# Rotary embedding on one core: both products of a chunk in one VectorE operation, and four units stored in two transfers of 64 partitions

## Chip, cores and metric

One core of a Trainium2 chip. The metric is device time in microseconds (us); lower is better. A run's time is some 2 us longer than the span that its profile shows (85.87 against 83.8 in the profiled run of before).

## The reference

```python
batch, n_heads, seq, head_dim = (8, 8, 1024, 64)        # fp32
x_first, x_second = x[..., :32], x[..., 32:]
out_first  = x_first * cos_cached - x_second * sin_cached
out_second = x_first * sin_cached + x_second * cos_cached
```

The input is 16.8 MB and the output another 16.8 MB. Every element is read once, takes part in two products and one sum, and is written once.

## The kernel before

The data is cut into eight units of 2 MB, each 128 partitions by 64 rows of 64 values (16 KB per partition). All eight loads go out at the start, on SyncE's queue, and the stores follow on the same queue in the order 0, 1, 3, 2, 4, 5, 6, 7. ScalarE copies a chunk of 24 or 16 rows into PSUM (`st`). VectorE multiplies the copy by the sines into `s` and by the cosines into `x`. The sums are shared out: TensorE (accumulating in PSUM, copied back by ScalarE), GpSimd, or VectorE itself in the chunks called `alone`. GpSimd does unit 2 alone.

```python
xt = [xp.tile([P, F], fp32, name=f"x{u}") for u in range(n_u)]
# ... cut: unit 0 is loaded in two halves of its columns
for u in range(1, n_u):
    nc.sync.dma_start(out=xt[u], in_=xf[u])
# ... cut
def products(pt, u, n0, n1, alone=False):
    xr, sr, pr = rows(xt[u], n0, n1), rows(s_of(u), n0, n1), rows(pt, 0, n1 - n0)
    mul(nc.vector, sr, pr, tab(sn, n0, n1))
    mul(nc.vector, pr if alone else xr, pr, tab(cs, n0, n1))
    if alone:
        sums(nc.vector, xr, pr, sr)

def store(u, n0=0, n1=R):
    nc.sync.dma_start(out=of[u][:, n0 * hd:n1 * hd], in_=xt[u][:, n0 * hd:n1 * hd])
# ... cut
for c, (u, n0, n1) in enumerate(chunks):
    products(st[c], u, n0, n1, (u, n0) in alone)
    put(c + 2)                       # ScalarE stages the chunk after next
    if c in back:
        pe_back(*back[c])            # sums of TensorE back into x
    if c in on_pe:
        pe_sums(*on_pe[c])
    for f, *args in behind.get(c, ()):
        f(*args)                     # GpSimd's sums, and the stores
```

Of the kernel before, what the change touches and what calls it, by code (L numbers as in the profile page):

```python
# [8 lines left out]
def kernel(  # L9
# [7 lines left out]
    nc = tc.nc  # L17
    fp32 = mybir.dt.float32
    TT = mybir.AluOpType
    P = nc.NUM_PARTITIONS  # L20

    b, h, seq, hd = x.shape
    half = hd // 2
    R = 64
    F = R * hd
    T = R * half
    n_u = (b * h * seq) // (R * P)
    BK = 512
    G = BK // half
    Q = 32  # L30
    H = R // 2
    C = H * half
# [4 lines left out]
    of = out.rearrange("b h s d -> (b h s d)").rearrange(  # L37
        "(u p m) -> u p m", p=P, m=F)

    ctx.enter_context(tc.manual_schedule())  # L40
    const = ctx.enter_context(tc.tile_pool(name="const", bufs=1))
    xp = ctx.enter_context(tc.tile_pool(name="xp", bufs=1))
    tv = ctx.enter_context(tc.tile_pool(name="tv", bufs=3))
    tg = ctx.enter_context(tc.tile_pool(name="tg", bufs=1))

    cs = const.tile([P, T], fp32, name="cs")
    sn = const.tile([P, T], fp32, name="sn")
    ones = const.tile([P, 2 * P], fp32, name="ones")
    sel, plus = ones[0:Q, :P], ones[:, P:]
    minus = const.tile([P, P], fp32, name="minus")  # L50


    raw = tv.tile([P, F], fp32, name="raw", tag="s")
    rs, rc = raw[0:Q, 0:C], raw[0:Q, C:2 * C]
    nc.sync.dma_start(out=rs, in_=sin_cached.rearrange("(q n) j -> q (n j)", q=Q))
    nc.scalar.dma_start(out=rc, in_=cos_cached.rearrange("(q n) j -> q (n j)", q=Q))


    xt = [xp.tile([P, F], fp32, name=f"x{u}") for u in range(n_u)]
    for m0, m1 in ((0, F // 2), (F // 2, F)):  # L60
        nc.sync.dma_start(out=xt[0][:, m0:m1], in_=xf[0][:, m0:m1])
    for u in range(1, n_u):
# [7 lines left out]
                            channel_multiplier=1)  # L70
    nc.gpsimd.affine_select(out=plus, in_=plus, compare_op=TT.not_equal, fill=1.0,
                            base=0, pattern=[[-1, P]], channel_multiplier=1)
    nc.vector.tensor_scalar_mul(out=minus, in0=plus, scalar1=-1.0)

    def rows(t, n0, n1):
        return t[:, n0 * hd:n1 * hd].rearrange("p (n k j) -> p n k j", k=2, j=half)

    def tab(t, n0, n1):
        v = t[:, n0 * half:n1 * half].rearrange("p (n o j) -> p n o j", o=1, j=half)
        return v.to_broadcast([P, n1 - n0, 2, half])  # L80

    def mul(eng, o, a, t):
        eng.tensor_tensor(out=o, in0=a, in1=t, op=TT.mult)  # L83

    def sums(eng, o, c, s):
        eng.tensor_tensor(out=o[:, :, 0], in0=c[:, :, 0], in1=s[:, :, 1], op=TT.subtract)  # L86
        eng.tensor_tensor(out=o[:, :, 1], in0=c[:, :, 1], in1=s[:, :, 0], op=TT.add)  # L87

    sv = {}

    def s_of(u):
        if u not in sv:
            sv[u] = tv.tile([P, F], fp32, name="s", tag="s")
        return sv[u]

    def stage(pt, u, n0, n1):
        nc.scalar.copy(out=pt[:, :(n1 - n0) * hd], in_=xt[u][:, n0 * hd:n1 * hd])  # L97

    def products(pt, u, n0, n1, alone=False):

        xr, sr, pr = rows(xt[u], n0, n1), rows(s_of(u), n0, n1), rows(pt, 0, n1 - n0)
        mul(nc.vector, sr, pr, tab(sn, n0, n1))
        mul(nc.vector, pr if alone else xr, pr, tab(cs, n0, n1))
        if alone:
            sums(nc.vector, xr, pr, sr)

    def on_pool(u, n0, n1):
        g = tg.tile([P, F // 2], fp32, name="g")
        xr, gr = rows(xt[u], n0, n1), rows(g, 0, n1 - n0)
        mul(nc.gpsimd, gr, xr, tab(sn, n0, n1))  # L110
        mul(nc.gpsimd, xr, xr, tab(cs, n0, n1))
        sums(nc.gpsimd, xr, xr, gr)

    def pool_sums(u, n0, n1):
        xr = rows(xt[u], n0, n1)
        sums(nc.gpsimd, xr, xr, rows(s_of(u), n0, n1))

    def store(u, n0=0, n1=R):
        nc.sync.dma_start(out=of[u][:, n0 * hd:n1 * hd], in_=xt[u][:, n0 * hd:n1 * hd])



# [2 lines left out]
    with ExitStack() as first:  # L125
        p0, p1 = [first.enter_context(tc.tile_pool(name=n, bufs=1, space=PS))
                  for n in ("p0", "p1")]
        en = p0.tile([P, C], fp32, name="en")
        ec = [p0.tile([P, BK], fp32, name=f"ec{i}") for i in range(2)]
        pre = p1.tile([P, 4 * BK], fp32, name="pre")  # L130
        for part, r in ((en[:, :BK], rs[:, :BK]), (en[:, BK:], rs[:, BK:]),
                        (ec[0], rc[:, :BK]), (ec[1], rc[:, BK:])):
            nc.tensor.matmul(part, sel, r, start=True, stop=True)  # L133
        odd = [2 * (i % (Q // 2)) + 1 for i in range(Q)]
        for t, r in ((sn, rs), (cs, rc)):
            nc.vector.stream_shuffle(t[0:Q, C:], r, odd)  # L136
        for t in (sn, cs):
            for k in range(1, P // Q):
                nc.gpsimd.tensor_copy(out=t[k * Q:(k + 1) * Q, C:], in_=t[0:Q, C:])  # L139
        mul(nc.vector, rows(s_of(0), 0, H), rows(xt[0], 0, H), tab(en, 0, H))  # L140
        for i in range(2):
            xr = rows(xt[0], i * G, (i + 1) * G)
            mul(nc.vector, xr, xr, tab(ec[i], 0, G))
        pool_sums(0, 0, H)
        stage(pre, 0, H, R)
        nc.scalar.copy(out=sn[:, :C], in_=en)
        for i in range(2):
            nc.scalar.copy(out=cs[:, i * BK:(i + 1) * BK], in_=ec[i])
        products(pre, 0, H, R)
        pool_sums(0, H, R)  # L150

# [2 lines left out]
    st, acc = {}, {}  # L154

    def pe_sums(u, n0):
        acc[u, n0] = q2.tile([P, 2 * BK], fp32, name="acc")
        a = acc[u, n0].rearrange("p (k n j) -> p k n j", k=2, j=half)
        xr, sr = rows(xt[u], n0, n0 + G), rows(s_of(u), n0, n0 + G)
        for k in range(2):  # L160
            nc.tensor.matmul(a[:, k], plus, xr[:, :, k], start=True, stop=False)  # L161
            nc.tensor.matmul(a[:, k], plus if k else minus, sr[:, :, 1 - k],  # L162
                             start=False, stop=True)

    def pe_back(u, n0):
        a = acc[u, n0].rearrange("p (k n j) -> p n k j", k=2, j=half)
        nc.scalar.copy(out=rows(xt[u], n0, n0 + G), in_=a)  # L167

    on_pool(2, 0, 32)


    cuts = ((0, 24), (24, 48), (48, 64))
    chunks = [(u, n0, n1) for u in (1, 3, 4, 5, 6, 7) for n0, n1 in cuts]
    alone = {(1, 48), (3, 48), (6, 48), (7, 24), (7, 48)}
    on_pe = {0: (1, 0), 1: (1, 16), 3: (3, 0), 4: (3, 16), 6: (3, 32), 8: (4, 0),
             9: (5, 0), 11: (5, 16), 12: (6, 0)}
    back = {1: (1, 0), 3: (1, 16), 4: (3, 0), 6: (3, 16), 8: (3, 32), 9: (4, 0),
            11: (5, 0), 12: (5, 16), 14: (6, 0)}
    behind = {
        1: [(pool_sums, 1, 32, 48), (on_pool, 2, 32, 64)],  # L180
        3: [(store, 1)],
        8: [(store, 3), (store, 2), (pool_sums, 4, 16, 64)],
        9: [(store, 4)],
        11: [(pool_sums, 5, 32, 64)],
        12: [(store, 5)],
        13: [(pool_sums, 6, 16, 48)],
        14: [(store, 6)],
        15: [(pool_sums, 7, 0, 24)],
        16: [(store, 7, 0, 48)],
        17: [(store, 7, 48, 64)],  # L190
    }

    def put(c):
        if c < len(chunks):
            u, n0, n1 = chunks[c]
            st[c] = (q1 if c % 2 else q0).tile([P, 3 * BK], fp32, name="st")
            stage(st[c], u, n0, n1)
# [2 lines left out]
    put(1)  # L200
    store(0)
    for c, (u, n0, n1) in enumerate(chunks):
        products(st[c], u, n0, n1, (u, n0) in alone)
        put(c + 2)
        if c in back:
            pe_back(*back[c])
# [3 lines that stand above are left out]
            f(*args)  # L210
# [29 lines left out]
```

## Time and profile before

| | before |
|---|---|
| time, median of 6 runs | 85.78 us (85.73 to 85.88) |
| span of the profiled run | 83.8 us |
| busy: VectorE, GpSimd, ScalarE | 72.3, 65.9, 37.2 us |
| DMA, share of 16 engines, main queue | 95.7% |
| last VectorE operation ends, last store lands | 77.3, 82.7 us |

Two rows disagree on what the bound is: VectorE is busy 86% of the span and the page's chain of work ends on it, while the DMA engines are busy longer and to the end. In a table of stretches, the last two columns are the mean busy share of the 16 DMA engines and the GB/s they moved. A packet is what the profile records as one piece of a DMA engine's work: of the 2640 in the main queue before, 1792 are the 16 KB that a unit has on one partition.

### The profile page before, as it was taken

The numbers are of one execution on the slowest core, as the hardware profiler recorded it, in microseconds if no ns is written. First come the engines' busy times: TensorE is split into PE (matmuls) and PEld (weight loads), VectorE is DVE, ScalarE is ACT, GpSimd is POOL, SyncE is SP. The second block draws the span as 40 slices with busy tenths as digits, with TensorE's granted clock in tenths as the row PEclk, the third lists the DMA queues.
The fourth block names the chain that finished last, engine by engine and source line by source line (L and its number), as shares of the span: only waits on it lengthen the run. The fifth ranks groups of instructions, "written<-read, shape, count | busy, mean of one in ns | idle before, by whom it ended". The sixth has DMA issues, their size and how long they took to land. (4 is left out here: it accounts for less than half of the span.)

```text
span 83.8 us, 409 instructions
## 1 busy us (share of the span) xinstructions
PE 42.4 (51%) x80; PEld 16.2 (19%) x80; DVE 72.3 (86%) x56; ACT 37.2 (44%) x32; POOL 65.9 (79%) x35
## 2 busy tenths in 40 slices
PE   0299910003994965949469089594959800000000
PEld 0234100002341403314033042231404200000000
DVE  1284999999999999999999999999999999998000
ACT  4100694464066553674636951976346852000000
POOL 5059959999999999999999999999999959400000
PEclk9999999999999999999999999999999999655555
DMA  2999999999999999999999999999999999999990
GB/s 59 309 411 450 415 461 391 461 415 454 415 415 454 399 469 399 446 422 415 352 415 446 415 446 407 462 415 446 422 422 454 399 450 407 462 415 434 417 385 23
DMA packets 2689, 33.83 MB, mean 404 GB/s; under 512 B 320, under 2 KB 320, under 8 KB 512
## 3 DMA queue, kind: packets, MB, share of 16 engines
q1 hardware_dynamic: 2640, 33.69, 95.7%
q10 hardware_dynamic: 48, 0.13, 0.4%
q14 instruction: 1, 0.01, 0.0%
HBM read 17.04 MB, written 16.78 MB: 404 GB/s over the span
## 5 line engine op out<-in xcount | busy, mean ns | idle before, releaser
L97 ACT COPY st<-x 128x1536 f32<-128x1536 f32 (+1 forms) x18 | 23.4, 1302 | 18.2 <-DVE x L83 10.2
L161 PE MATMUL acc<-x,ones 128*128 128x512 f32 x36 | 20.4, 650 | 20.6 <-ACT x L167 11.3
L83 DVE TENSOR_TENSOR s<-st,sn 128x1536 f32<-128x1536 f32 (+1 forms) x18 | 28.2, 1568 | 0.0
L83 DVE TENSOR_TENSOR x<-st,cs 128x1536 f32<-128x1536 f32 (+1 forms) x13 | 21.6, 1663 | 0.0
L86 POOL TENSOR_TENSOR x<-x,s 128x1024 f32<-128x1024 f32 (+3 forms) x7 | 15.8, 2262 | 1.9 <-ACT x L167 0.9
L87 POOL TENSOR_TENSOR x<-x,s 128x1024 f32<-128x1024 f32 (+3 forms) x7 | 15.8, 2258 | 0.0
L161 PEld LDWEIGHTS acc<-x,ones 128*128 128x128 f32 x36 | 6.6, 204 | 33.6 <-ACT x L167 17.9
L167 ACT COPY x<-acc 128x1024 f32<-128x1024 f32 x9 | 9.1, 1010 | 6.5 <-PE acc L162 6.5
L162 PE MATMUL acc<-s,minus 128*128 128x512 f32 x18 | 10.1, 644 | 0.0
L83 POOL TENSOR_TENSOR x<-x,cs 128x2048 f32<-128x2048 f32 x2 | 9.1, 4540 | 0.2
L162 PE MATMUL acc<-s,ones 128*128 128x512 f32 x18 | 9.2, 592 | 0.0
L83 POOL TENSOR_TENSOR g<-x,sn 128x2048 f32<-128x2048 f32 x2 | 9.1, 4532 | 0.0
L83 DVE TENSOR_TENSOR st<-st,cs 128x1024 f32<-128x1024 f32 (+1 forms) x5 | 6.6, 1328 | 0.0
L139 POOL COPY sn<-sn 32x1024 f32<-32x1024 f32 x3 | 3.1, 1032 | 3.4 <-DVE sn L136 3.3
L133 PE MATMUL en<-raw,ones 32*128 32x512 f32 x4 | 3.7, 1089 | 3.7 <-DMA raw<-in_sin_cached_dram 3.7
L86 POOL TENSOR_TENSOR x<-x,g 128x1024 f32<-128x1024 f32 x2 | 4.7, 2350 | 0.2
L97 ACT COPY pre<-x 128x2048 f32<-128x2048 f32 x1 | 1.9, 1870 | 6.6 <-DMA x<-in_x_dram 6.6
L87 POOL TENSOR_TENSOR x<-x,g 128x1024 f32<-128x1024 f32 x2 | 4.7, 2358 | 0.0
L162 PEld LDWEIGHTS acc<-s,minus 128*128 128x128 f32 x18 | 3.7, 206 | 4.9 <-issue 4.9
L162 PEld LDWEIGHTS acc<-s,ones 128*128 128x128 f32 x18 | 3.4, 190 | 4.3 <-issue 4.3
L86 DVE TENSOR_TENSOR x<-st,s 128x512 f32<-128x512 f32 (+1 forms) x5 | 3.7, 745 | 0.2
L87 DVE TENSOR_TENSOR x<-st,s 128x512 f32<-128x512 f32 (+1 forms) x5 | 3.7, 733 | 0.0
(23 smaller groups left out, 25.9 us busy)
## 6 DMA issues: line engine op xcount, KB each, us to landing
x<-in_x_dram SPq DMA_DIRECT2D x7, 2048.0 KB, 24.8
out_dram<-x SPq DMA_DIRECT2D x7, 2048.0 KB, 10.1
x<-in_x_dram SPq DMA_DIRECT2D x2, 1024.0 KB, 6.4
out_dram<-x SPq DMA_DIRECT2D x1, 1536.0 KB, 7.7
out_dram<-x SPq DMA_DIRECT2D x1, 512.0 KB, 5.4
raw<-in_cos_cached_dram ACTq DMA_DIRECT2D x1, 128.0 KB, 3.2
raw<-in_sin_cached_dram SPq DMA_DIRECT2D x1, 128.0 KB, 2.8
```

The source lines that it names most:

```text
L83: eng.tensor_tensor(out=o, in0=a, in1=t, op=TT.mult)
L86: eng.tensor_tensor(out=o[:, :, 0], in0=c[:, :, 0], in1=s[:, :, 1], op=TT.subtract)
L87: eng.tensor_tensor(out=o[:, :, 1], in0=c[:, :, 1], in1=s[:, :, 0], op=TT.add)
L97: nc.scalar.copy(out=pt[:, :(n1 - n0) * hd], in_=xt[u][:, n0 * hd:n1 * hd])
L133: nc.tensor.matmul(part, sel, r, start=True, stop=True)
L139: nc.gpsimd.tensor_copy(out=t[k * Q:(k + 1) * Q, C:], in_=t[0:Q, C:])
L161: nc.tensor.matmul(a[:, k], plus, xr[:, :, k], start=True, stop=False)
L162: nc.tensor.matmul(a[:, k], plus if k else minus, sr[:, :, 1 - k], start=False, stop=True)
L167: nc.scalar.copy(out=rows(xt[u], n0, n0 + G), in_=a)
```

## The change

The intent is to take VectorE's fixed cost per instruction (some 65 ns by the starts in the trace of before: 1.67 us apart at 1536 elements, 1.13 at 1024) once per chunk in place of twice. To let one operation write both products, `x` and `s` of a unit become neighbours in one wide tile, cosine and sine tables are interleaved row by row, and pairs of units share a product buffer. Work is rebalanced: unit 2 goes partly to VectorE, and two of the five `alone` chunks give their sums away. Separately, the first four stores are cut in two. The core of the diff:

```diff
+    for i, (u0, u1) in enumerate(((3, 6), (0, 4), (1, 5))):
+        w = xp.tile([P, 3 * F], fp32, name=f"w{i}")
+        xt[u0], xt[u1] = w[:, :F], w[:, 2 * F:]
+        sv[u0] = sv[u1] = w[:, F:2 * F]
+        px[u0], px[u1] = both(w[:, :2 * F]), both(w[:, F:])[:, :, ::-1]
 ... cut: units 7 and 2, tables, order of the work
-        mul(nc.vector, sr, pr, tab(sn, n0, n1))
-        mul(nc.vector, pr if alone else xr, pr, tab(cs, n0, n1))
+        mul(nc.vector, px[u][:, n0:n1].rearrange("p n t (k j) -> p n t k j", k=2),
+            xr.to_broadcast([P, n, 2, hd]).rearrange("p n t (k j) -> p n t k j", k=2), tr)
 ... cut
-        nc.sync.dma_start(out=of[u][:, n0 * hd:n1 * hd], in_=xt[u][:, n0 * hd:n1 * hd])
+        step = P // 2 if u < 4 else P
+        for p in range(0, P, step):
+            nc.sync.dma_start(out=of[u][p:p + step, n0 * hd:n1 * hd],
+                              in_=xt[u][p:p + step, n0 * hd:n1 * hd])
```

More of the change, by code (lines that the diff above doesn't have):

```diff
@@ L42 @@
     xp = ctx.enter_context(tc.tile_pool(name="xp", bufs=1))
-    tv = ctx.enter_context(tc.tile_pool(name="tv", bufs=3))
-    tg = ctx.enter_context(tc.tile_pool(name="tg", bufs=1))
-    cs = const.tile([P, T], fp32, name="cs")
-    sn = const.tile([P, T], fp32, name="sn")
+    tb = const.tile([P, 2 * T], fp32, name="tb")
+    tb4 = tb.rearrange("p (n t j) -> p n t j", t=2, j=half)
     ones = const.tile([P, 2 * P], fp32, name="ones")
@@ L50, with both @@
     minus = const.tile([P, P], fp32, name="minus")
-    raw = tv.tile([P, F], fp32, name="raw", tag="s")
-    rs, rc = raw[0:Q, 0:C], raw[0:Q, C:2 * C]
+    xt, sv, px = {}, {}, {}
+    def both(t):
+        return t.rearrange("p (w n f) -> p n w f", w=2, f=hd)
+    for i, (u0, u1) in enumerate(((3, 6), (0, 4), (1, 5))):
[3 more added lines that the diff above has]
+        px[u0], px[u1] = both(w[:, :2 * F]), both(w[:, F:])[:, :, ::-1]
+    K = 40
+    w = xp.tile([P, K * hd + F], fp32, name="w3")
+    gt, xt[7] = w[:, :K * hd], w[:, K * hd:]
+    sv[7], px[7] = gt, both(w[:, :2 * K * hd])[:, :, ::-1]
+    xt[2], sv[2] = xp.tile([P, F], fp32, name="x2"), sv[3]
+    rs, rc = sv[3][0:Q, 0:C], sv[3][0:Q, C:2 * C]
     nc.sync.dma_start(out=rs, in_=sin_cached.rearrange("(q n) j -> q (n j)", q=Q))
     nc.scalar.dma_start(out=rc, in_=cos_cached.rearrange("(q n) j -> q (n j)", q=Q))
-    xt = [xp.tile([P, F], fp32, name=f"x{u}") for u in range(n_u)]
     for m0, m1 in ((0, F // 2), (F // 2, F)):
@@ L72 @@
                             base=0, pattern=[[-1, P]], channel_multiplier=1)
-    nc.vector.tensor_scalar_mul(out=minus, in0=plus, scalar1=-1.0)
+    nc.scalar.mul(out=minus, in_=plus, mul=-1.0)
+    cs, sn = tb4[:, :, 0], tb4[:, :, 1]
     def rows(t, n0, n1):
@@ L78, in tab, with flat @@
     def tab(t, n0, n1):
-        v = t[:, n0 * half:n1 * half].rearrange("p (n o j) -> p n o j", o=1, j=half)
-        return v.to_broadcast([P, n1 - n0, 2, half])
+        return t[:, n0:n1].unsqueeze(2).to_broadcast([P, n1 - n0, 2, half])
+    def flat(t):
+        return t.rearrange("p (n j) -> p n j", j=half)
     def mul(eng, o, a, t):
@@ L87, in sums, with products, alone @@
         eng.tensor_tensor(out=o[:, :, 1], in0=c[:, :, 1], in1=s[:, :, 0], op=TT.add)
-    sv = {}
-    def s_of(u):
-        if u not in sv:
-            sv[u] = tv.tile([P, F], fp32, name="s", tag="s")
-        return sv[u]
     def stage(pt, u, n0, n1):
         nc.scalar.copy(out=pt[:, :(n1 - n0) * hd], in_=xt[u][:, n0 * hd:n1 * hd])
-    def products(pt, u, n0, n1, alone=False):
-        xr, sr, pr = rows(xt[u], n0, n1), rows(s_of(u), n0, n1), rows(pt, 0, n1 - n0)
+    def products(pt, u, n0, n1):
+        n = n1 - n0
+        if u not in px:
+            for o, t in ((sv[u], sn), (xt[u], cs)):
+                mul(nc.vector, rows(o, n0, n1), rows(pt, 0, n), tab(t, n0, n1))
+            return
+        xr = pt[:, :n * hd].rearrange("p (n o f) -> p n o f", o=1, f=hd)
+        tr = tb4[:, n0:n1].unsqueeze(3).to_broadcast([P, n, 2, 2, half])
+        mul(nc.vector, px[u][:, n0:n1].rearrange("p n t (k j) -> p n t k j", k=2),
+            xr.to_broadcast([P, n, 2, hd]).rearrange("p n t (k j) -> p n t k j", k=2), tr)
+    def alone(pt, u, n0, n1):
+        s = sv[4] if u == 7 else sv[u]
+        xr, sr, pr = rows(xt[u], n0, n1), rows(s, n0, n1), rows(pt, 0, n1 - n0)
         mul(nc.vector, sr, pr, tab(sn, n0, n1))
-        mul(nc.vector, pr if alone else xr, pr, tab(cs, n0, n1))
-        if alone:
-            sums(nc.vector, xr, pr, sr)
+        mul(nc.vector, pr, pr, tab(cs, n0, n1))
+        sums(nc.vector, xr, pr, sr)
     def on_pool(u, n0, n1):
-        g = tg.tile([P, F // 2], fp32, name="g")
-        xr, gr = rows(xt[u], n0, n1), rows(g, 0, n1 - n0)
+        xr, gr = rows(xt[u], n0, n1), rows(gt, n0, n1)
         mul(nc.gpsimd, gr, xr, tab(sn, n0, n1))
@@ L115, in pool_sums @@
         xr = rows(xt[u], n0, n1)
-        sums(nc.gpsimd, xr, xr, rows(s_of(u), n0, n1))
+        sums(nc.gpsimd, xr, xr, rows(sv[u], n0, n1))
     def store(u, n0=0, n1=R):
-        nc.sync.dma_start(out=of[u][:, n0 * hd:n1 * hd], in_=xt[u][:, n0 * hd:n1 * hd])
+        step = P // 2 if u < 4 else P
+        for p in range(0, P, step):
+            nc.sync.dma_start(out=of[u][p:p + step, n0 * hd:n1 * hd],
+                              in_=xt[u][p:p + step, n0 * hd:n1 * hd])
     PS = bass.MemoryType.PSUM
@@ L135 @@
         for t, r in ((sn, rs), (cs, rc)):
-            nc.vector.stream_shuffle(t[0:Q, C:], r, odd)
-        for t in (sn, cs):
-            for k in range(1, P // Q):
-                nc.gpsimd.tensor_copy(out=t[k * Q:(k + 1) * Q, C:], in_=t[0:Q, C:])
-        mul(nc.vector, rows(s_of(0), 0, H), rows(xt[0], 0, H), tab(en, 0, H))
+            nc.vector.stream_shuffle(t[0:Q, H:], flat(r), odd)
+        for k in range(1, P // Q):
+            nc.gpsimd.tensor_copy(out=tb4[k * Q:(k + 1) * Q, H:], in_=tb4[0:Q, H:])
+        mul(nc.vector, rows(sv[0], 0, H), rows(xt[0], 0, H), tab(flat(en), 0, H))
         for i in range(2):
             xr = rows(xt[0], i * G, (i + 1) * G)
-            mul(nc.vector, xr, xr, tab(ec[i], 0, G))
+            mul(nc.vector, xr, xr, tab(flat(ec[i]), 0, G))
         pool_sums(0, 0, H)
         stage(pre, 0, H, R)
-        nc.scalar.copy(out=sn[:, :C], in_=en)
+        nc.scalar.copy(out=sn[:, :H], in_=flat(en))
         for i in range(2):
-            nc.scalar.copy(out=cs[:, i * BK:(i + 1) * BK], in_=ec[i])
+            nc.scalar.copy(out=cs[:, i * G:(i + 1) * G], in_=flat(ec[i]))
         products(pre, 0, H, R)
@@ L158, in pe_sums @@
         a = acc[u, n0].rearrange("p (k n j) -> p k n j", k=2, j=half)
-        xr, sr = rows(xt[u], n0, n0 + G), rows(s_of(u), n0, n0 + G)
+        xr, sr = rows(xt[u], n0, n0 + G), rows(sv[u], n0, n0 + G)
         for k in range(2):
@@ L167, in pe_back @@
         nc.scalar.copy(out=rows(xt[u], n0, n0 + G), in_=a)
-    on_pool(2, 0, 32)
+    on_pool(2, 0, K // 2)
     cuts = ((0, 24), (24, 48), (48, 64))
     chunks = [(u, n0, n1) for u in (1, 3, 4, 5, 6, 7) for n0, n1 in cuts]
-    alone = {(1, 48), (3, 48), (6, 48), (7, 24), (7, 48)}
-    on_pe = {0: (1, 0), 1: (1, 16), 3: (3, 0), 4: (3, 16), 6: (3, 32), 8: (4, 0),
-             9: (5, 0), 11: (5, 16), 12: (6, 0)}
-    back = {1: (1, 0), 3: (1, 16), 4: (3, 0), 6: (3, 16), 8: (3, 32), 9: (4, 0),
-            11: (5, 0), 12: (5, 16), 14: (6, 0)}
-    behind = {
-        1: [(pool_sums, 1, 32, 48), (on_pool, 2, 32, 64)],
-        3: [(store, 1)],
-        8: [(store, 3), (store, 2), (pool_sums, 4, 16, 64)],
-        9: [(store, 4)],
-        11: [(pool_sums, 5, 32, 64)],
-        12: [(store, 5)],
-        13: [(pool_sums, 6, 16, 48)],
-        14: [(store, 6)],
-        15: [(pool_sums, 7, 0, 24)],
-        16: [(store, 7, 0, 48)],
-        17: [(store, 7, 48, 64)],
+    chunks.insert(9, (2, K, R))
+    whole = {(6, 48), (7, 24), (7, 48)}
+    on_pe = {0: (1, 0), 3: (3, 0), 4: (3, 16), 6: (4, 0), 7: (4, 16), 10: (5, 0),
+             11: (5, 16), 13: (6, 0)}
+    back = {2: (1, 0), 4: (3, 0), 6: (3, 16), 8: (4, 0), 9: (4, 16), 11: (5, 0),
+            13: (5, 16), 15: (6, 0)}
+    behind = {
+        2: [(pool_sums, 1, 16, 64), (store, 1)],
+        5: [(pool_sums, 3, 32, 64), (on_pool, 2, K // 2, K)],
+        6: [(store, 3)],
+        9: [(pool_sums, 2, K, 64), (store, 2), (pool_sums, 4, 32, 64), (store, 4)],
+        12: [(pool_sums, 5, 32, 64)],
+        13: [(store, 5)],
+        14: [(pool_sums, 6, 16, 48)],
+        15: [(store, 6)],
+        16: [(pool_sums, 7, 0, 24)],
+        17: [(store, 7, 0, 48)],
+        18: [(store, 7, 48, 64)],
     }
@@ L202 @@
     for c, (u, n0, n1) in enumerate(chunks):
-        products(st[c], u, n0, n1, (u, n0) in alone)
+        (alone if (u, n0) in whole else products)(st[c], u, n0, n1)
         put(c + 2)
```

## The prediction

A is the rival in which the stores in halves run at half the rate; its "up to 105" is 85.8 + 19.6, and its "95 to 102" stands as the author's guess.

> **What bounds the kernel now.** I read the page's chain of work that ended last first, because it names a culprit, and then tried to refute it.
>
> ```profile
> DVE 38%; issue 2%; DVEq 1%
> DVE s L83 17%; DVE x L83 13%; DVE st L83 5%; DVE x L86 2%; DVE x L87 2%; DVEq L235 1%
> ```
>
> The chain ends on VectorE and never mentions a transfer. Taken at its word, each microsecond saved on VectorE would be a microsecond of the kernel. But the chain only reaches back to 42 us and covers 41% of the span, and VectorE's last operation ends at 77.3 us while the span is 83.8. So I looked at what the transfers do, in the slices and in the queue part of the page.
>
> ```profile
> DVE  1284999999999999999999999999999999998000
> DMA  2999999999999999999999999999999999999990
> GB/s 59 309 411 450 415 461 391 461 415 454 415 415 454 399 469 399 446 422 415 352 415 446 415 446 407 462 415 446 422 422 454 399 450 407 462 415 434 417 385 23
> q1 hardware_dynamic: 2640, 33.69, 95.7%
> HBM read 17.04 MB, written 16.78 MB: 404 GB/s over the span
> ```
>
> Both rows are full, but only the DMA row is full until the end. All loads and all stores are in one queue (q1), which holds 95.7% of the time of 16 engines. The table of stretches gives the rate:
>
> ```profile
> 2.50:37.00 34.50, 20.17 (x32) 7.59 (x32) 31.84 (x25) 15.96 (x14) 30.69 (x16) 1.00 1.02 427
> 37.00:44.00 7.00, 5.16 (x12) 2.18 (x13) 7.00 (x6) 3.59 (x5) 6.92 (x3) 1.00 0.99 396
> 44.00:81.00 37.00, 17.04 (x38) 6.44 (x36) 33.21 (x26) 16.32 (x14) 27.19 (x11) 0.88 1.00 428
> ```
>
> The last two columns are the DMA share and GB/s: 427 while loading, 428 while storing, share 1.0 in both. Last, does the queue ever wait for a store? The time line of SyncE and the waits of the stores, one at a time, give issue and time to landing. The first store is issued at 21.58 us and lands 27.0 us later, because the loads queue ahead of it (the last load, issued at 6.5, lands after 37.1, at 43.6). The last one:
>
> ```profile
> 77.34 0.33 SPq L119 DMA_DIRECT2D out_dram<-x  x1
> DMA to landing us min/median/max: 5.4/5.4/5.4
> ```
>
> Issue plus landing for all nine: unit 0 at 21.6 lands 48.6; 1 at 37.9 lands 53.4; 3 at 48.5 lands 58.2; 2 at 51.7 lands 63.1; 4 at 58.5 lands 68.0; 5 at 63.1 lands 73.0; 6 at 67.8 lands 77.9; 7a at 73.8 lands 81.5; 7b at 77.3 lands 82.7. Whole units land 4.8 to 5.0 us apart (2.10 MB at 428 GB/s is 4.90), and every store is issued 4 us or more before the one ahead of it has landed (the least: 73.8 against 77.9). The queue never runs dry. **The bound is the transfers' rate**, and VectorE is second with about 3 us of slack: 4 us less roughly 1 us from issue to the first byte (the first load is issued at 1.2; traffic is seen from about 2).
>
> [...]starts lie 1.67 us apart at 1536 elements and 1.13 at 1024, so 1.04 to 1.05 ns per element and some 65 ns fixed. [...]each 2 MB transfer spans 128 partitions, and the two 32-partition loads are 128 KB, too small to show a rate.
>
> **The change part by part.**
> VectorE: 15 chunks and the second half of unit 0 become one operation of double length in place of two, 16 x 65 ns = -1.0 us. Two "alone" chunks lose their two sums, 0.69 and 0.68 us with the gap around 1.3: -2.7. One chunk of unit 2 (24 rows) comes over from GpSimd as two operations of 1.67: +3.3. Sum -0.4: the last operation would end near 76.9 instead of 77.3. The negated identity moves to ScalarE: 0.23 us at 1.7 us, where VectorE waited anyway: 0.
> GpSimd: unit 2 costs 4.53 + 4.54 + 2.35 + 2.36 = 13.8 us per 32 rows; 40 rows instead of 64 save 10.3. Its sums grow from 216 to 288 rows, at 2 x 2.34 us per 32 rows: +10.5. Sum about 0. TensorE loses one group of nine and ScalarE one copy out of PSUM (1.0), for one staging copy (1.44): 0.
> Store times by the new order: unit 3 near 42 (behind sums of GpSimd), 2 near 54, 4 near 58.5, 5 near 63, 6 near 68, 7a near 73.2, 7b near 77. Only unit 2 moves back, by 2 us, and it is not wanted before unit 3 has landed, at 58. So the queue still never runs dry, and all of the VectorE part is **worth 0 on the path**.
> Transfers: same bytes. Units 0, 1, 2, 3 take eight transfers in place of four; the four further issues, 0.33 us each on SyncE, lie far ahead of need. So 8.4 MB, or 4 x 4.9 = 19.6 us of the path, run in a new form, and its rate is the one term that can move the time much. If each engine still moves 16 KB rows at its own pace, the term is 0. What could be won is the weak stretch from loads to stores: 37 to 44 us at 396 GB/s instead of 427, 7 x 31/427 = 0.5 us. Half of that, -0.3, is my guess, as someone who split only the first four stores was probably looking there.
> Sum: 85.84 + 0 + 0 - 0.3 = 85.5.
>
> **The rivals.**
> A, [...]19.6 us become up to 39, and since queue time is path time, the kernel would take up to 105 us; [...]less, 95 to 102. Against it: [...]the restriction to four units looks like a choice made after trying. I give it about 1 in 5.
> B, VectorE was the bound after all, as the chain has it. Then the time falls by its 0.4 us: 85.4. Hardly to be told apart from my number; a landing well after issue speaks against it.
> C, a new wait. One fused operation writes two tiles, and units now share product buffers: the chunk of unit 2 (VectorE ready near 42.6) needs the sums of unit 3 done by GpSimd (near 41.7), less than 1 us of margin; if ordering is kept by whole buffers, other chunks might wait too. Waits below 3 us in total vanish in the slack; 5 us would give 88. About 1 in 12. A slower rate of the fused operation, whose output jumps between two regions, would act alike: 10% on 16 operations of 3.2 us is 5 us.
> D, the transition and the end both get tighter: 0.5 us from above, and 0.8 at most from engines that finish unevenly (81 to 82.7 us runs at a falling rate). That gives 84.5. Below 84.1, which 2% takes, there is nothing left to win, as the bytes alone at 428 GB/s take 78.7 us, and the start and the end of the program are unchanged.
>
> **Range and chances.** Between D and a small C lie 84.5 and 87; A lies far outside, and I leave it there. Faster by over 2%: 0.05, as D falls short of it. Slower by over 2%: 0.22, almost all A and some C. Within 2%: 0.73. Predicted 85.5, range 84.4 to 87.2.
>
> **What would show it.** Right: VectorE's last operation near 77, last store's issue near 77, landing near 82.5, DMA share 1.0 and over 420 GB/s in 44 to 64 us, a fused operation of 3072 elements near 3.27 us from start to start. A: in the stretch where units 0 to 3 leave, share near 1.0 at 220 to 300 GB/s, units landing 7 to 10 us apart, GpSimd and VectorE unchanged. C: gaps on VectorE named after GpSimd or TensorE and, only then, DMA slices below 9. The prediction is wrong if the time leaves 2%, and its reasoning is wrong if VectorE ends much earlier and the time follows it.

## The result, and the profile after

The changed kernel takes 99.44 us (median of 6 runs, 97.35 to 101.03) against 85.78: ratio 1.142, 95% interval 1.133 to 1.151. A ratio here is the mean time of one kernel's fast runs over that of the other's fast runs of the same rounds, so not quite the ratio of the medians. The time scatters by 4%, where before it scattered by 0.2%. Runs more than 1.5% above the fastest are labelled slow: four of the six here. The fast ones are 97.35 and 98.64 us; the second is the profiled one (span 96.2).

The prediction's main number was wrong. Its rival A had foreseen 95 to 102 us, at a chance of 1 in 5.

VectorE, transfers and rate in 40 slices, from the page of after (a slice is 2.4 us, 2.1 before):

```profile
DVE  0367999999999999999999999999999910000000
DMA  2999999999999999999979989999999999998410
GB/s 37 381 409 480 436 429 422 422 402 415 429 422 436 436 436 436 436 402 375 252 232 211 347 259 279 354 375 395 286 293 354 415 429 429 412 431 366 208 77 12
```

The DMA row stays full, but the rate falls to between 211 and 395 GB/s from the twentieth slice to the thirtieth (46 to 72 us). That is where units 0 to 3 leave. Then it recovers, and at the very end it fades over four slices where before it stopped in one. The table of stretches of after, columns as in the prediction's:

```profile
2.50:37.00 34.50, 19.12 (x27) 7.17 (x28) 31.56 (x15) 16.64 (x15) 29.81 (x13) 0.97 1.02 427
44.00:60.00 16.00, 11.91 (x26) 4.31 (x24) 16.00 (x7) 10.31 (x10) 15.84 (x9) 1.00 1.01 275
84.00:96.20 12.20, 0.00 (x0) 0.00 (x0) 0.00 (x0) 0.00 (x0) 0.00 (x0) 0.50 0.53 224
```

Loading runs at the old 427 GB/s. From 44 to 60 us the share is 1.01 at 275 GB/s: the engines always have a packet in hand, and the packets are slow. The records of single 16 KB packets say so directly: 0.61 us nearly everywhere before (some thirty of 1792 took up to 1.08 us, most of them at the turn from loads to stores), and a mixture of 0.61, 1.2 and up to 1.5 us here, with four up to 2.7.

From the time line of VectorE and the waits of SyncE, after and then before:

```profile
76.61 0.68 DVE L108 TENSOR_TENSOR w<-st,w 128x512 f32<-128x512 f32 x1
SPq L263 <- DMA out_dram<-w: 17.5, 5, 4.8
```
```profile
SPq L235 <- DMA out_dram<-x: 5.0, 2, 3.8
```

VectorE ends at 77.3 us as before, and the last store is issued at 77.3 as before. It then takes 18.1 us to land instead of 5.4, and SyncE waits 17.5 us for transfers at the end. The end of the computation did not move; the queue behind it did. Whole units, which had landed every 4.9 us, are complete at 50.2, 58.8, 65.8 and 76.0 us (units 0, 1, 3, 2), and from there every 4.8 us again.

Of the 12.4 us of longer span, part is an uneven finish of the engines: in the last 12.2 us they idle 0.47 x 12.2 = 5.7 us on the mean, where the last 7.8 us before had 0.28 x 7.8 = 2.2. That is 3.5 us; the other 8.9 are slower packets.

### The profile page after: what moved, and what is told of

Read it like the earlier page. It is cut to its first block, busy times and chain, and to the rows that moved or that the text cites. A ratio compares the mean times of both kernels' runs of the same rounds, so it can differ in the third digit from the quotient of the medians.

```text
span 96.2 us, 376 instructions
## 1 busy us (share of the span) xinstructions
PE 40.6 (42%) x72; PEld 15.4 (16%) x72; DVE 71.7 (75%) x37; ACT 37.8 (39%) x33; POOL 65.9 (68%) x36
## 5 line engine op out<-in xcount | busy, mean ns | idle before, releaser
L104 DVE TENSOR_TENSOR w<-st,tb 128x3072 f32<-128x3072 f32 (+3 forms) x19 | 50.6, 2727 | 0.0
L111 ACT COPY st<-w 128x1536 f32<-128x1536 f32 (+1 forms) x18 | 23.4, 1302 | 20.6 <-DVE w L104 14.9
L188 PE MATMUL acc<-w,ones 128*128 128x512 f32 x32 | 19.4, 693 | 19.5 <-ACT w L194 10.4
L107 POOL TENSOR_TENSOR w<-w 128x1024 f32<-128x1024 f32 (+2 forms) x8 | 19.3, 2418 | 0.4 <-POOL tb L166 0.4
L108 POOL TENSOR_TENSOR w<-w 128x1024 f32<-128x1024 f32 (+2 forms) x8 | 19.4, 2420 | 0.0
L188 PEld LDWEIGHTS acc<-w,ones 128*128 128x128 f32 x32 | 6.2, 215 | 31.7 <-ACT w L194 16.2
L189 PE MATMUL acc<-w,minus 128*128 128x512 f32 x16 | 10.0, 709 | 0.0
L194 ACT COPY w<-acc 128x1024 f32<-128x1024 f32 x8 | 8.1, 1009 | 3.5 <-PE acc L189 3.4
L189 PE MATMUL acc<-w,ones 128*128 128x512 f32 x16 | 8.2, 592 | 0.0
L104 POOL TENSOR_TENSOR x<-x,tb 128x1280 f32<-128x1280 f32 x2 | 5.8, 2898 | 0.2
L104 POOL TENSOR_TENSOR w<-x,tb 128x1280 f32<-128x1280 f32 x2 | 5.9, 2947 | 0.0
L107 POOL TENSOR_TENSOR x<-x,w 128x640 f32<-128x640 f32 (+1 forms) x3 | 4.9, 1636 | 0.2
L108 POOL TENSOR_TENSOR x<-x,w 128x640 f32<-128x640 f32 (+1 forms) x3 | 4.9, 1636 | 0.0
L189 PEld LDWEIGHTS acc<-w,ones 128*128 128x128 f32 x16 | 3.1, 193 | 4.2 <-issue 4.2
## 6 DMA issues: line engine op xcount, KB each, us to landing
out_dram<-w SPq DMA_DIRECT2D x1, 512.0 KB, 18.1
```

The lines of the kernel that those rows point to most:

```text
L104: eng.tensor_tensor(out=o, in0=a, in1=t, op=TT.mult)
L107: eng.tensor_tensor(out=o[:, :, 0], in0=c[:, :, 0], in1=s[:, :, 1], op=TT.subtract)
L108: eng.tensor_tensor(out=o[:, :, 1], in0=c[:, :, 1], in1=s[:, :, 0], op=TT.add)
L111: nc.scalar.copy(out=pt[:, :(n1 - n0) * hd], in_=xt[u][:, n0 * hd:n1 * hd])
L188: nc.tensor.matmul(a[:, k], plus, xr[:, :, k], start=True, stop=False)
L189: nc.tensor.matmul(a[:, k], plus if k else minus, sr[:, :, 1 - k], start=False, stop=True)
```

## The experiments

**Theory P** (partitions): stores that take partitions 0 to 63 and 64 to 127 of SBUF, the on-chip memory, in separate transfers are slow because of which partitions they take, and all of the loss is there; the VectorE part is worth nothing, because the transfers are the bound. The mechanism that P assumed behind this was shown by no run. Rivals: the new layout (L), the number of transfers (N), the order of the writes in HBM (H), and the moment (T, U). Except where said, an experiment edits the kernel *before*, so that nothing else differs; "before" was 85.80 to 85.83 us beside all of them (a single run of it, of 172 us, was a disturbance).

| run | median us | ratio (95%) |
|---|---|---|
| e1, change without the split | 85.94 | 1.002 (0.997 to 1.006) |
| e2, split alone | 98.93 | 1.140 (1.130 to 1.150) |
| e3, split by columns | 85.93 | 0.999 (0.995 to 1.003) |
| e4, same half twice | 104.47 | 1.217 (1.211 to 1.222) |
| e5, split of unit 0 only | 88.33 | 1.030 (1.028 to 1.032) |
| e6, split of the last four | 95.02 | 1.108 (1.105 to 1.111) |
| e8, even and odd partitions | 85.56 | 0.999 (0.995 to 1.003) |
| e9, loads in halves | 105.24 | 1.227 (1.225 to 1.229) |
| e10, VectorE one operation more | 86.19 | 1.005 (0.998 to 1.013) |
| e11, VectorE four more | 92.07 | 1.068 (1.061 to 1.076) |
| e12, middle half twice | 85.68 | 0.996 (0.990 to 1.003) |
| e13, change with even and odd | 100.73 | 1.173 (1.165 to 1.180) |

Medians are of all runs, ratios of the fast ones alone. Labelled slow are two of the four runs of e2 and one each of e11 and e12. The fast runs of e2 (97.34 and 98.56, mean 97.95) stand against a mean of 85.94 for before, so the split costs 12.0 us by fast runs.

### Which part costs: e1 and e2

e1, in the changed kernel:
```diff
-        step = P // 2 if u < 4 else P
+        step = P
```

> The changed kernel with every store again one transfer of 128 partitions; the fused VectorE operation, the new buffers and the new order stay. Theory P ([...]the VectorE part is worth nothing because the queue of transfers is the bound): 85.4 to 86.0 us, ratio to before 0.995 to 1.003, 425 GB/s or more from 44 to 81 us, VectorE still ending near 77. Rival L (the new layout, fused writes that jump between two regions, or shared buffers slow the stores): 97 to 100 us, as the whole change.

e2, in the kernel before:
```diff
+        step = P // 2 if u < 4 else P
+        for p in range(0, P, step):
+            nc.sync.dma_start(out=of[u][p:p + step, n0 * hd:n1 * hd],
+                              in_=xt[u][p:p + step, n0 * hd:n1 * hd])
-        nc.sync.dma_start(out=of[u][:, n0 * hd:n1 * hd], in_=xt[u][:, n0 * hd:n1 * hd])
```

> The kernel before with nothing changed but the stores of units 0 to 3, each in two transfers of 64 partitions. Theory P: 96 to 102 us, all of the change's loss, 16 KB packets stretched from 0.61 to 1.2 us or more in the stretch where these units leave, 230 to 350 GB/s there. Rival L: 85.5 to 86.5.

Both as P expects. e1 gives 85.94, e2 98.93, the changed kernel 99.44. Stretches of e1, then of e2:

```profile
44.00:76.00 32.00, 16.04 (x35) 5.94 (x33) 31.93 (x18) 16.09 (x14) 27.92 (x14) 0.89 1.00 429
```
```profile
46.00:60.00 14.00, 9.48 (x22) 3.74 (x21) 14.00 (x10) 9.23 (x8) 13.92 (x6) 1.00 1.00 287
```

With the fused operation and whole stores the transfers keep 429 GB/s. With the old computation and split stores they fall to 287 at a full share. Rival L is out, and the two parts of the change are separated: the VectorE part brings 0, the split brings all of the loss. e1 does not say which engine is the bound: in its trace VectorE ended no earlier (77.92 against 77.32), so that it could gain nothing either way. That is left to e10 and e11.

### Two transfers, or these two: e3

```diff
+        cut = (n0 + n1) // 2 if u < 4 else n1
+        for m0, m1 in ((n0, cut), (cut, n1)):
+            if m1 > m0:
+                nc.sync.dma_start(out=of[u][:, m0 * hd:m1 * hd], in_=xt[u][:, m0 * hd:m1 * hd])
```

> The kernel before with the stores of units 0 to 3 each in two transfers as well, but cut by columns: 128 partitions of 8 KB each. Theory P: 85.7 to 86.4 us, as every transfer again spans all partitions; only the smaller packets cost a little (8 KB in about 0.308 us, two of them 0.616 against 0.611). Rival N (the number of transfers, their issue or their completion is what costs): 95 us or more, like the split by partitions.

85.93 us, ratio 0.999. The same number of transfers of the same size costs nothing if each spans 128 partitions. Its stretch while these units leave, at 431 GB/s:

```profile
44.00:64.00 20.00, 14.38 (x33) 5.56 (x32) 19.97 (x15) 12.63 (x11) 19.92 (x8) 1.00 1.02 431
```

Rival N is out.

### SBUF side or HBM side: e4 and e12

e4 (wrong result):
```diff
             nc.sync.dma_start(out=of[u][p:p + step, n0 * hd:n1 * hd],
-                              in_=xt[u][p:p + step, n0 * hd:n1 * hd])
+                              in_=xt[u][0:step, n0 * hd:n1 * hd])
```

> Wrong result on purpose: as the split alone, with the same destinations in HBM, but the second transfer of each pair reads partitions 0 to 63 again, not 64 to 127. Theory P: [...]the four units run at half rate all through: four times 4.9 us more, 103 to 107 us, slower than the split alone, packets of 1.2 us and more, 205 to 230 GB/s over some 39 us. Rival H (the loss is on the HBM side, from the order in which 64 rows are written): the same time as the split alone, within 1.5 us.

e12 (wrong result): the same with `in_=xt[u][32:96, ...]` for both transfers of units 0 to 3.

> Wrong result on purpose: as the same half twice, but both transfers of each of units 0 to 3 read partitions 32 to 95, a contiguous half[...]. [...]85.5 to 86.5 us, as with even and odd partitions, packets 0.61 us. If any contiguous 64 partitions are slow: 103 to 105, as the same half twice.[...]

The destinations in HBM are those of e2 in both. Only the partitions read differ. e4 takes 104.47 us, 5.5 more than e2; e12 takes 85.68, as if nothing had been split. The rate of e4 by slices and in a stretch, then of e12 in the same stretch:

```profile
GB/s 61 371 422 451 435 416 416 442 442 435 416 410 448 435 435 416 410 326 205 205 205 205 218 211 211 205 205 218 205 208 211 282 429 416 422 448 429 426 387 77
46.00:60.00 14.00, 9.54 (x18) 3.44 (x16) 12.57 (x10) 8.13 (x7) 13.92 (x6) 0.88 1.00 207
```
```profile
46.00:60.00 14.00, 9.48 (x18) 3.65 (x18) 12.59 (x10) 8.23 (x8) 13.92 (x6) 0.88 1.01 431
```

A flat 205 to 218 GB/s for some 33 us, with every 16 KB packet from 46 to 60 us at 1.2 to 1.29 us, twice 0.61. The share of 1.00 also shows that all 16 engines were at work; half of them alone would show 0.5. The contiguous 64 partitions from 32 to 95 run at 431. So the HBM side (H) is out, and so are the number 64 and contiguity as such. What counts is *which* partitions: 0 to 63 ran at 207 GB/s, 32 to 95 at 431. What in the chip makes the difference, no record here shows.

e2, in which lower and upper halves alternate, is less slow than e4: 287 GB/s against 207 in the same stretch. The packets agree: from 46 to 60 us e4 has none below 1.0 us, e2 has many at 0.61 beside some of 1.5. Why some packets of e2 keep their pace was not shown; the packet records kept here carry no engine's name.

### How the loss grows: e5 and e6

As e2, with `u == 0` and with `u >= 4` as the condition.

> The kernel before with only the first store (unit 0) in two transfers of 64 partitions. Theory P: the loss comes per unit stored this way. One unit read at half rate costs up to 4.9 us; I expect 88 to 91 us. Rival U (an unlucky one-time event at the change from loads to stores is what costs, and any split store there starts it): most of the 12 us at once, 94 or more.[...]

> The kernel before with the split moved to the other half: units 4 to 7 in two transfers of 64 partitions, units 0 to 3 whole. Theory P: it does not matter when the halves are stored, 94 to 101 us; perhaps a little less than the split of the first four, as the last stores leave no later transfers to carry the engines' uneven ends. Rival T (only stores queued beside loads suffer): 85.7 to 87.

88.33 and 95.02 us, both in the range that P expected. Slices of e5, then a stretch of e6 before and after unit 4 begins to leave:

```profile
GB/s 63 306 418 445 456 396 472 396 456 403 449 403 449 411 441 411 441 434 418 358 456 243 205 403 418 449 411 441 411 449 411 449 407 449 411 449 409 417 363 29
```
```profile
44.00:64.00 20.00, 14.38 (x33) 5.57 (x32) 20.00 (x15) 12.44 (x11) 19.92 (x8) 1.00 1.02 430
64.00:83.00 19.00, 3.00 (x7) 0.98 (x6) 13.56 (x13) 4.04 (x4) 7.66 (x4) 0.68 0.99 293
```

One split unit makes a dip of two slices (243, 205) and costs 2.5 us; then the old rate returns. Stores that leave 20 us after the last load suffer as well. So it is neither a one-time event (U) nor the nearness of the loads (T). The last four cost 9.2 us, the first four 12.0 by fast runs. I had expected a little less there, with no whole stores left behind them; the size of the gap isn't explained further.

A detail that P doesn't give by itself: in e4 and e5 the first half to leave runs at full rate (packets of 0.61 to 0.77 us from 42.5 to 44.7 us in e4, 426 GB/s from 42.0 to 44.5 us in e5), and the slowing begins with the second. So e5 pays for one half, not for two: by an estimate, its 64 packets are 4 for each of 16 engines, at 1.24 - 0.61 = 0.63 us more each (the packets of e4), 2.5 us. Why the first half is spared was not tested. In e6, where the halves follow whole stores, the rate from 63 to 66 us is already down to 311 GB/s.

### Which 64 partitions: e8

```diff
+        if u < 4:
+            for p in range(2):
+                nc.sync.dma_start(out=of[u][p::2, n0 * hd:n1 * hd],
+                                  in_=xt[u][p::2, n0 * hd:n1 * hd])
+            return
```

> The kernel before with units 0 to 3 each stored in two transfers of 64 partitions, the even ones and the odd ones. [...]slower than before, less slow than the halves, 88 to 96 us. If the number of partitions in a transfer (64) is all that counts: 96 to 100. If only a contiguous half is bad: 85.7 to 86.5.

A miss: 85.56 us, ratio 0.999, every 16 KB packet from 46 to 60 us at 0.61 to 0.64 us.

```profile
46.00:60.00 14.00, 9.47 (x22) 3.65 (x21) 14.00 (x10) 9.24 (x8) 13.92 (x6) 1.00 1.01 431
```

The number lies near the third alternative, that only a contiguous half is bad; e12 rules that one out. The loss of 88 to 96 us that I expected rested on an assumption about the engines' shares that no trace shows; no loss is seen. What e2, e4, e8 and e12 leave standing is what they measured: 207 GB/s for partitions 0 to 63 alone, 287 for lower and upper halves in turn, 431 for 32 to 95 and for every second one. e8 and e12 both take 32 partitions from 0 to 63 and 32 from 64 to 127; whether 64 to 127 alone are as slow as 0 to 63 was not tested.

### The other direction: e9

```diff
     for u in range(1, n_u):
-        nc.sync.dma_start(out=xt[u], in_=xf[u])
+        step = P // 2 if u >= 4 else P
+        for p in range(0, P, step):
+            nc.sync.dma_start(out=xt[u][p:p + step], in_=xf[u][p:p + step])
```

> The kernel before with its stores, but the loads of units 4 to 7 each in two transfers of 64 partitions. Theory P holds for both directions[...]: 94 to 106 us, rate in the later loads between 200 and 330 GB/s. If only reading SBUF is limited so: 85.7 to 86.5.

105.24 us. The stretch in which units 4 to 7 arrive:

```profile
26.00:60.00 34.00, 24.64 (x50) 9.22 (x48) 32.53 (x24) 20.20 (x18) 33.69 (x13) 0.95 1.00 212
```

212 GB/s at a full share, flat, although lower and upper halves alternate as in e2. The loss is 105.2 - 85.8 = 19.4 us, just the four units' 4 x 4.9 once more. So loads pay in full and stores (12.0 us) only in part; why is open.

### Was VectorE really off the path? e10 and e11

```diff
+        for _ in range(1 if (u, n0) == (6, 0) else 0):      # e11: 4
+            mul(nc.vector, rows(s_of(u), n0, n1), rows(st[c], 0, n1 - n0), tab(sn, n0, n1))
         products(st[c], u, n0, n1, (u, n0) in alone)
```

> The kernel before with one VectorE product of unit 6 done twice (same result): 1.67 us more on VectorE, ahead of the last three stores. If the queue of transfers is the bound with about 3 us of slack behind VectorE, as the prediction has it: 85.7 to 86.3 us, the last store issued near 79.0 and landing near 82.7 as before. If VectorE is the bound, as the chain of waits suggests: 87.5 us.

> The same product done five times: 6.67 us more on VectorE. With 3 us of slack: 85.8 + 6.7 - 3.1 = 89.4 us (88.8 to 90.0), and a visible gap of the transfers before the stores of units 6 and 7. With VectorE as the bound: 92.5 us. If there is more slack than I think: below 88.8.

e10 gave 86.19 us (85.82 to 87.04), its median within its range. e11 gave 92.07, above its range and near the number of the rival that makes VectorE the bound. The traces say why the simple sum failed. In both, VectorE also waited for a copy of ScalarE. That wait in e10, and the start of the last VectorE operation in before, e10 and e11:

```profile
DVE s L83 <- ACT st L97: 1.3, 1, 1.3
```
```profile
76.64 0.68 DVE L87 TENSOR_TENSOR x<-st,s 128x512 f32<-128x512 f32 x1
```
```profile
79.92 0.68 DVE L87 TENSOR_TENSOR x<-st,s 128x512 f32<-128x512 f32 x1
```
```profile
85.65 0.68 DVE L87 TENSOR_TENSOR x<-st,s 128x512 f32<-128x512 f32 x1
```

The added operations did not cause the wait. It ends at 56.35 us in e10, before the first of them starts, and e12 and e4, which add none, have it too (1.4 us each). What these four traces share is the clock granted to TensorE: 0.57 to 0.66 from 48 to 52 us, against 1.00 in before. A pair of matmuls took 2.07 us in place of 1.12 there (e10), ScalarE waited 3.4 us for TensorE's sums in place of 1.8, and its next copy for VectorE was late.

So the last operation of e10 starts 3.3 us later, not 1.7; the span grew by 0.7 (84.5 against 83.8). In e11 the wait is 1.4 us, the repeated products start 1.77 us apart in place of 1.67, and the last operation starts 9.0 us later; the span grew by 6.4 (90.2; that run, of 92.29 us, is labelled slow against the fastest of 90.84; two others took 92.06 and 92.08). 3.3 - 0.7 and 9.0 - 6.4 are both **2.6 us: that is the slack behind VectorE in these two traces**, against the 3 of the prediction. Seen from the last store: in before it lands 5.4 us after its issue, in both of these 2.8 us after it, though it is issued 5.8 us later in e11 than in e10 (86.4 against 80.6). Two of the four runs of e10 took 85.82 us, no longer than before; they were not profiled. e11 shows what it looks like when the queue does run dry, with holes in both rows:

```profile
DMA  2999999899899899999999989999950992885992
GB/s 29 320 418 476 385 465 450 363 465 458 363 458 458 371 450 465 385 429 465 421 392 465 458 371 450 465 400 414 465 233 0 414 400 120 341 356 233 436 374 120
```

### The change, mended: e13

In the changed kernel, the two transfers of units 0 to 3 take `p::2` as in e8.

> The whole change with one thing mended: the two transfers of units 0 to 3 take the even and the odd partitions in place of the lower and the upper half. Theory P[...]: 85.5 to 86.1 us, no loss and, as the bytes and the rate are the bound, no gain over the kernel before either.

A second miss, and for a new reason: 100.73 us, correct. Rate by slices, and waits of VectorE:

```profile
GB/s 45 371 425 435 425 425 425 425 425 425 425 425 425 425 425 432 439 445 425 425 439 53 319 425 106 0 0 80 412 419 445 346 405 432 13 425 425 249 412 189
DVE w L104 <- DMA out_dram<-w: 17.5, 2, 14.1
48.46 8.82 DVE L104 TENSOR_TENSOR w<-st,tb 128x3072 f32<-128x3072 f32 x3 [14.10 <-DMA out_dram<-w]
```

Where the transfers run they run at 425 GB/s, with nearly all packets at 0.61 to 0.65 us: slow packets are not the trouble. But VectorE stood still for 14.1 us, until the store of unit 0 had landed (48.2), before it wrote the first chunk of unit 4, and 3.4 us later on in the same way, for the store of unit 3. Its last operation ends at 94.96, 17.6 us later than before; less the slack of 2.6, that is 15.0 us, and the kernel lost 14.9. Units 0 and 4 share one wide tile in the new layout; the store reads unit 0's columns, the chunk writes others. In e1, whose instructions are the same on all engines but SyncE, there is no such wait. So storing every second partition out of a shared tile makes the program keep an order that the bytes do not need. Why it does was not tested. It is the kind of wait of the prediction's rival C ("if ordering is kept by whole buffers"), brought in by the mending.

No version beat the kernel before by more than the scatter. With 427 to 431 GB/s in nearly every stretch of before, and 16 KB packets that took 0.61 us at best (the shortest 0.608 us in before, 0.611 in after), there was little left to win.

## Why the prediction was wrong

- **The bound: right.** Transfers are the bound. In e10 and e11 VectorE could end 2.6 us later before the span grew, against "about 3". That e1 gains nothing is no evidence, as VectorE ended no earlier in it. The chain of waits, which named VectorE, would have misled.
- **VectorE part, "worth 0 on the path": right**, with its terms. Fused operations of 3072 elements start 3.27 us apart, as predicted. The 65 ns per instruction nearly hold too: two operations of 1536 elements took 3.33 us from start to start before (16.52 to 19.85), so one of 3072 saves 0.06. From its first table product to its last operation's end VectorE takes 69.5 us (7.81 to 77.29) against 69.9 before (7.46 to 77.32): -0.4, as predicted; it shows no earlier end because the work began 0.35 us later in this trace. GpSimd is busy 65.9 us in both. e1 shows a ratio of 1.002.
- **Transfers, "in a new form, and its rate is the one term that can move the time much": right. Its size, "the term is 0" and the guess of -0.3: the step that failed.** Four units whose rate was taken as unchanged ran at 287 GB/s in place of 428 (e2, 46 to 60 us) and cost 12.0 us. The further issues, put at 0.33 us each, took up to 2.45 us on SyncE, but the last store was still issued at 77.3. Rival A had the half rate that e4 shows (207 GB/s of 431), the range (95 to 102; e2 gave 98.9, the whole change 99.4) and even the partial relief (e2: 287 GB/s), without which e4 takes 104.5.
- **Why it was mis-sized.** No trace that I had showed a large transfer on half of the partitions, so its rate was open. I took it as unchanged, and against A I set a guess about the author: that splitting just four stores "looks like a choice made after trying". That is no evidence on the chip, and could not carry odds of 1 in 5.
- **C and D.** No new wait in the changed kernel: VectorE's idle time in the main loop is 0. The weak stretch from loads to stores did not get tighter in a way that mattered.

## What to carry to other kernels

When the transfers are the bound, ask of every transfer which partitions it reaches, not only how many bytes and how many transfers it has: partitions 0 to 63 moved at about half the rate (207 GB/s, e4) of 32 to 95 or of every second one (431, e12 and e8). Tell slow packets from missing ones by holding the DMA share against the GB/s. And do not let a guess about why someone wrote a line stand in for a measurement: the rate that was taken as unchanged here was 287 GB/s in place of 428.
